# The output projection of a hybrid decoder step as seven block products instead of eight, with combined weights made on GpSimd

## The chip, the core and the metric

The kernel runs on one NeuronCore of a Trainium2 chip. The metric is device time in microseconds, the median of several executions; lower is better. The engines that matter here: TensorE (PE in the profile) multiplies, VectorE (DVE) and ScalarE (ACT) do elementwise work, GpSimd (POOL) does masks and memsets, and SyncE (SP) issues nearly all DMAs, in one queue, in order. On an engine an instruction that waits holds up all behind it.

## The reference, cut to what matters

One decoder layer: a combined input projection, a stick-breaking attention group and a gated linear attention (GLA) group, a SiLU gate on each, one output projection over the concatenated 2048 features, an RMS norm and a residual. There are 1024 prompt tokens (behind 16 meta tokens, whose output isn't returned) and 8 x 4 sample tokens.

```python
def branch_output(o_sb, sg, o_gla, gg, gla_norm_g, w_out):
    ...
    mixed = jnp.concatenate([o_sb * jax.nn.silu(sg), o_gla * jax.nn.silu(gg)], axis=-1)
    return mixed @ w_out
...
        x = x + rms_norm(branch_output(o_sb, sg, o_gla, gg, gla_norm_g[l], w_out[l]), norm_post_g[l])
```

`mixed @ w_out` is a product of 1024 (+ 32 sample) rows, 2048 features and 2048 columns in float32. The change is about this product.

## The kernel before, in words

Float32 operands are split into a rounded high part and a remainder, and each product is made of three matmuls: high by high, high by low, low by high.

On TensorE follow: input projections and attention of 8 heads (`head`, `attend`), then the GLA groups, then the paged values of the samples, with the 16 gate groups (`gate_group`) in between. A gate group multiplies by a weight block, applies SiLU, multiplies by the branch output and stores 128 features of the mixed activations for all tokens in a DRAM buffer `md[g]` (L402). The last two gate groups, 14 and 15, stand directly ahead of the output projection.

Side work is written as Python generators that a `Weaver` advances: each `W.beat()` in the main loop lets due generators emit their next instructions; `yield n` and `spawn(gen, delay)` count beats, and a beat of the input projections is six matmuls. The place on an engine's queue is then settled, when the program is built, by a scheduler that takes priorities (`urgent()`) and its own idea of when operands are ready. During the heads the generator `z_feed` has VectorE multiply 512 pages of cached keys by the sample queries (L376), paced at one page every two beats; GpSimd then only masks the diagonal attention tiles (L488, L504).

The output projection runs over two halves of 512 tokens (the first with the 32 samples as 544 columns). For each of 16 blocks of 128 output columns and each pair of feature blocks, `weight_chunk` loads 128 x 256 weights (L177, through three buffers), ScalarE rounds them (L181) and VectorE makes the remainder (L182). Weights are stationary, the activations of the half (`mix`, 272 or 512 tokens wide) stream past them (L1269 to L1271). `y_tok` transposes each finished block back to token rows (L1207), takes squares and multiplies by the gain. `finish0` adds the residual of the first half and stores it (L1233 to L1236) while the second half is multiplied; `finish1` does so for the second half (L1260, L1262), in two groups of tokens, for which the last two column blocks are kept back.

## Time and profile before

| | us |
|---|---|
| median of 3 runs | 2215.75 (2213.62 to 2221.52) |
| profiled execution | 2214.65 |
| span of that execution | 2212.9 |
| TensorE busy | 2150.0 (97%) |
| VectorE busy | 1593.0 (72%) |
| ScalarE busy | 1059.4 (48%) |
| GpSimd busy | 87.2 (4%) |

The span is what the profile covers; the time of the same execution is 1.75 us longer. Matmuls overlap, and their ends are modelled, so the sum of their durations isn't the time that they cost: the distance between starts is. A row of the groups reads: line, engine, operation, output<-inputs, shapes, count | busy us, mean ns of one | idle time of the engine just before them, and what ended most of it. A row of a stretch reads: start and end, length, busy us (and instructions) of PE, PEld (weight loads), DVE, ACT and POOL, the clock that TensorE was granted, the mean busy share of the 16 DMA engines, GB/s. A row of the chain reads: start, length, what; the chain follows the work that ended last back to what released it. A row of the timeline reads: start, length, engine, line, operation. SPq is SyncE's DMA queue.

### The profile page before, as it was taken

The numbers are of one execution on the slowest core, as the hardware profiler recorded it, in microseconds if no ns is written. First come the engines' busy times: TensorE is split into PE (matmuls) and PEld (weight loads), VectorE is DVE, ScalarE is ACT, GpSimd is POOL, SyncE is SP. The second block draws the span as 40 slices with busy tenths as digits, with TensorE's granted clock in tenths as the row PEclk, the third lists the DMA queues.
The fourth block names the chain that finished last, engine by engine and source line by source line (L and its number), as shares of the span: only waits on it lengthen the run. The fifth ranks groups of instructions, "written<-read, shape, count | busy, mean of one in ns | idle before, by whom it ended". The sixth has DMA issues, their size and how long they took to land. (4 is left out here: it accounts for less than half of the span.)

```text
span 2212.9 us, 46718 instructions
## 1 busy us (share of the span) xinstructions
PE 2150.0 (97%) x13712; PEld 1988.2 (90%) x13712; DVE 1593.0 (72%) x6809; ACT 1059.4 (48%) x2900; POOL 87.2 (4%) x299
## 2 busy tenths in 40 slices
...
GB/s 190 63 75 104 83 106 94 102 105 80 108 97 95 105 80 126 108 74 106 102 89 114 83 116 82 90 161 194 201 193 193 191 179 142 86 84 170 238 96 134
DMA packets 411299, 267.53 MB, mean 121 GB/s; under 512 B 49378, under 2 KB 393890, under 8 KB 409890
## 3 DMA queue, kind: packets, MB, share of 16 engines
...
q8 instruction: 108, 1.77, 0.3%
...
## 5 line engine op out<-in xcount | busy, mean ns | idle before, releaser
L376 DVE SCALAR_TENSOR_TENSOR jk<-kp,qb 128x128 f32<-128x128 f32 x2048 | 486.9, 287 | 40.9 <-DMA kp<-in_cache_k_dram 38.0
L286 PE MATMUL acc_g<-hT,wh_g 128*128 128x368 f32 (+2 forms) x768 | 258.0, 336 | 0.2
L287 PE MATMUL acc_g<-hT,wh_g 128*128 128x368 f32 (+2 forms) x768 | 247.6, 322 | 0.0
L288 PE MATMUL acc_g<-hT,wl_g 128*128 128x368 f32 (+2 forms) x768 | 246.9, 322 | 0.0
L1269 PE MATMUL oacc<-mx,wh_o 128*128 128x272 f32 (+1 forms) x736 | 238.8, 325 | 6.3 <-ACT wh_o L181 4.4
L1271 PE MATMUL oacc<-mx,wl_o 128*128 128x272 f32 (+1 forms) x736 | 235.5, 320 | 0.0
L1270 PE MATMUL oacc<-mx,wh_o 128*128 128x272 f32 (+1 forms) x736 | 234.8, 319 | 0.2 <-DVE mx L1186 0.2
L182 DVE TENSOR_TENSOR wl_o<-wr_o,wh_o 128x256 fp32r<-128x256 f32 x240 | 101.4, 425 | 152.4 <-ACT wh_o L181 146.3
L286 PEld LDWEIGHTS acc_g<-hT,wh_g 128*128 128x128 f32 x768 | 144.2, 188 | 33.6 <-issue 21.8
L376 DVE DVE_READ_ACCUMULATOR jk<-kp,qb 128x1 f32 x2048 | 166.0, 81 | 0.0
L181 ACT CAST wh_o<-wr_o 128x256 fp32r<-128x256 f32 x240 | 96.7, 405 | 138.7 <-PE oacc L1270 100.9
L1269 PEld LDWEIGHTS oacc<-mx,wh_o 128*128 128x128 f32 x736 | 139.1, 189 | 17.8 <-ACT wh_o L181 6.9
L1271 PEld LDWEIGHTS oacc<-mx,wl_o 128*128 128x128 f32 x736 | 138.6, 188 | 10.2 <-DVE wl_o L182 1.3
L1270 PEld LDWEIGHTS oacc<-mx,wh_o 128*128 128x128 f32 x736 | 138.9, 189 | 8.6 <-DVE mx L1186 0.5
L287 PEld LDWEIGHTS acc_g<-hT,wh_g 128*128 128x128 f32 x768 | 144.4, 188 | 1.1 <-issue 0.4
L288 PEld LDWEIGHTS acc_g<-hT,wl_g 128*128 128x128 f32 x768 | 144.3, 188 | 0.4 <-issue 0.4
L286 PE MATMUL acc_gv<-hT,wh_gv 128*128 128x384 f32 (+1 forms) x384 | 128.7, 335 | 0.0
L286 PE MATMUL acc_k<-hT,wh_k 128*128 128x378 f32 (+1 forms) x384 | 127.8, 333 | 0.0
L181 ACT CAST wh_g<-wr_g 128x256 fp32r<-128x256 f32 x128 | 51.7, 404 | 155.4 <-PE acc_g L287 140.1
L286 PE MATMUL acc_q<-hT,wh_q 128*128 128x368 f32 (+2 forms) x384 | 125.6, 327 | 0.0
L288 PE MATMUL acc_gv<-hT,wl_gv 128*128 128x384 f32 (+1 forms) x384 | 125.4, 327 | 0.0
L287 PE MATMUL acc_k<-hT,wh_k 128*128 128x378 f32 (+1 forms) x384 | 125.2, 326 | 0.0
(399 smaller groups left out, 5904.6 us busy)
## 6 DMA issues: line engine op xcount, KB each, us to landing
kp<-in_cache_k_dram SPq DMA_DIRECT2D x512, 64.0 KB
...
wr_o<-in_w_out_dram SPq DMA_DIRECT2D x256, 128.0 KB
...
wr_g<-in_w_in_dram SPq DMA_DIRECT2D x128, 128.0 KB
...
```

The lines of the kernel that those rows point to most:

```text
L181: act.copy(wh, raw[:])
L182: vec.tensor_tensor(wl, raw[:], wh.bitcast(F32), ALU.subtract)
L286: mm(acc[c][:, :n], wh[:, k2, :], hh[k][:, lo:hi], start=(k == 0), stop=False)
L287: mm(acc[c][:, :n], wh[:, k2, :], hl[k][:, lo:hi], start=False, stop=False)
L288: W.mark = mm(acc[c][:, :n], wl[:, k2, :], hh[k][:, lo:hi], start=False, stop=(k == NK - 1)).ins
L376: ins = vec.scalar_tensor_tensor(jk[:], kp[:], 1.0, qbs[h, b][:, t, :], ALU.mult, ALU.mult, accum_out=zt[:, t, NPG - 1 - i:NPG - i])
L1269: mm(o_, wh[:, k2, :], mh[:, lo:hi], start=(k == 0), stop=False)
L1270: mm(o_, wh[:, k2, :], ml[:, lo:hi], start=False, stop=False)
L1271: mm(o_, wl[:, k2, :], mh[:, lo:hi], start=False, stop=(k == NK - 1))
```

## The change

The output projection is now a block product by Strassen's method in Winograd's form. Activations A are cut into four quarters: two halves of 512 tokens by two halves of 1024 features; weights B into four quarters of 1024 features by 1024 columns. Seven products of a 512 x 1024 and a 1024 x 1024 matrix give what eight gave: 1 and 2 are quarters times quarters (A11 B11, A12 B21), 3 and 4 have a combined activation or weight, 5 to 7 have both. The sample rows don't take part: they are multiplied in the plain way, as 64 extra stationary columns (high and low parts of 32 rows), with the uncombined weight quarters that products 1, 2, 7 and 3 hold.

The parts:

- **Combined weights.** A new generator `weight_forms` starts 120 beats into the heads. In 16 rounds of 44 beats it loads four blocks of 128 x 512 weights (256 KB each), GpSimd makes four differences in place, and four blocks go out to DRAM buffers `td`. Each instruction is tied to the matmul emitted last (`spread`).
- **Gate groups 14 and 15** run ahead of the projection's pools, and the weight pool `wp` is closed after them; the projection's tiles are allocated anew. The sample columns of `md` are loaded early, as soon as a group is stored.
- **Forms.** `form(p)` loads the quarters of the activations that product p needs, combines them on VectorE (two of the sums are also stored and fetched again for later products), splits them and writes them over the slots of a finished product.
- **Products.** Activations are now stationary (128 features x 128 tokens) and weights stream, 512 columns wide. A `step(p, q)` is one product over one half of its columns: 8 feature blocks x 4 token tiles x 3 matmuls, into four PSUM banks of six in rotation. Weights come in chunks of 128 x 512 through three raw buffers and a ring of four split ones. The ring's index is the counter `turn`, which each `gain` load advances too (also in `sample_y`, which stands behind the steps of products 2 and 3).
- **Sums.** `take` adds a bank to the running sums in token rows; no transposes are left. Products 1 and 2 share banks, as do 6 and 7, and 5 and 3. The first token half is complete after product 3, and `finish0` and `finish_samples` are emitted from there on; the second half is complete with the fourth product, whose second column half has its weights kept (`kept`) and runs one token tile after another, each followed by `finish1`.

```diff
-    wp = ctx.enter_context(tc.tile_pool(name="wp", bufs=3))
+    wp_cm = tc.tile_pool(name="wp", bufs=3, side="right")
+    wp = wp_cm.__enter__()
...
+    td = [dram.tile([P, 8, 1024], F32, name=f"td{j}") for j in range(4)]
+    sd = [[dram.tile([P, 512], F32, name=f"sd{j}_{k}") for k in range(8)] for j in range(2)]
...
+    def spread(ins):
+        if W.mark is not None:
+            tc.add_manual_dep(ins.ins, W.mark.name, NOSYNC, reason="spread")
+    def weight_forms():
+        for k in range(8):
+            for q in range(2):
+                t = dk.tile([P, 4, 512], F32, tag="tf", bufs=1, name=f"tf{k}_{q}")
+                for i, (r, c) in enumerate(((0, 0), (0, 1), (1, 1), (1, 0))):
+                    r0, c0 = 1024 * r + k * P, 1024 * c + q * 512
+                    spread(nc.sync.dma_start(t[:, i, :], w_out[0, r0:r0 + P, c0:c0 + 512]))
+                    yield 4
+                yield 4
+                for i, a, b in ((0, 1, 0), (1, 1, 2), (2, 2, 0), (3, 3, 2)):
+                    spread(pool.tensor_tensor(t[:, i, :], t[:, a, :], t[:, b, :], ALU.subtract))
+                    yield 1
+                for j, i in enumerate((0, 2, 1, 3)):
+                    yield 4
+                    spread(nc.sync.dma_start(td[j][:, k, q * 512:(q + 1) * 512], t[:, i, :]))
...
         W.spawn(z_feed(lambda n: 2), lasting=True)
+        W.spawn(weight_forms(), 120, lasting=True)
         for h in range(HEADS):
...
+    small = [late.tile([P, 8, NSMP], F32, name=f"small{i}") for i in range(2)]
+    def load_small(c):
+        for k in range(8):
+            nc.sync.dma_start(small[c][:, k, :], md[8 * c + k][:, SEQ:TOUT])
+    gate_group(14)
+    load_small(0)
+    vec.tensor_tensor(small[0][:], small[0][:], osmp[:], ALU.mult)
+    gate_group(15)
+    wp_cm.__exit__(None, None, None)
...
+        REGION = dict(zip("ABC", ((0, 1, 2, 3), (6, 7, 8, 9), (10, 11, 12, 13))))
+        HOME = {1: "A", 2: "B", 6: "C", 7: "A", 5: "B", 3: "C", 4: "A"}
...
+        def quarter(r, c, k, nm):
+            t = raw(f"q{r}{c}_{k}_{nm}")
+            nc.sync.dma_start(t[:], md[8 * c + k][:, 512 * r:512 * r + 512])
+            return t[:]
...
+        def combined(p, k):
+            if p in (1, 2, 4):
+                return quarter(p == 4, p > 1, k, p)
+            if p == 6:
+                x, y_, z = quarter(1, 0, k, p), quarter(1, 1, k, p), quarter(0, 0, k, p)
+                vec.tensor_tensor(x, x, y_, ALU.add)
+                nc.sync.dma_start(sd[0][k][:], x)
+                vec.tensor_tensor(z, x, z, ALU.subtract)
+                nc.sync.dma_start(sd[1][k][:], z)
+                return z
+            if p == 5:
+                return stored(0, k)
+            x, y_ = (quarter(1, 0, k, p), quarter(0, 0, k, p)) if p == 7 else (quarter(0, 1, k, p), stored(1, k))
+            vec.tensor_tensor(x, x, y_, ALU.subtract)
+            return x
+        def form(p, gap):
+            sample = {1: 0, 2: 1, 7: 0, 3: 1}.get(p)
+            if p == 3:
+                vec.tensor_tensor(small[1][:], small[1][:], small[0][:], ALU.add)
+            for i in range(4):
+                t = slot(REGION[HOME[p]][i], f"f{p}_{i}")
+                for j in range(2):
+                    k = 2 * i + j
+                    f = t[:, j * 1024:(j + 1) * 1024].rearrange("p (s n) -> p s n", s=2)
+                    split(f[:, 0], f[:, 1], combined(p, k))
+                    forms[p, k] = f
+                    if sample is not None:
+                        f = t[:, 2048 + 64 * j:2112 + 64 * j]
+                        split(f[:, 0:NSMP], f[:, NSMP:64], small[sample][:, k, :])
+                        smp[p, k] = f
+                    if gap:
+                        yield gap
...
+        def weights(p, q, k, dst=None):
+            with urgent():
+                if dst is None:
+                    j = next(turn) % 4
+                    dst = [t[:, j * 512:(j + 1) * 512] for t in ring]
+                wh, wl = dst
+                r = op.tile([P, 512], F32, tag="wr", bufs=3, name=f"wr{p}{q}_{k}")[:]
+                if p <= 3:
+                    r0, c0 = (1024 if p > 1 else 0) + P * k, (1024 if p == 3 else 0) + 512 * q
+                    src = w_out[0, r0:r0 + P, c0:c0 + 512]
+                else:
+                    src = td[{5: 0, 6: 1, 7: 2, 4: 3}[p]][:, k, q * 512:(q + 1) * 512]
+                nc.sync.dma_start(r, src)
+                act.copy(wh, r)
+                vec.tensor_tensor(wl, r, wh.bitcast(F32), ALU.subtract)
+            return wh, wl
+        ring += [slot(4 + i, f"ring{i}") for i in range(2)]
+        for _ in form(1, 0):
+            pass
+        W.spawn(form(2, 1))
+        W.spawn(form(6, 3), 10)
...
+        def gain(b):
+            t = op.tile([P, 512], F32, tag="gpost", bufs=2, name=f"gpost{b}_{next(turn)}")
+            nc.sync.dma_start(t[:], norm_post_g[0, b * 512:(b + 1) * 512].partition_broadcast(P))
+            return t
...
+        def finish0():
+            r = scale((0, 1, 2, 3))
             for i in range(4):
+                for b in range(4):
+                    o = sums_[i, b]
+                    for f in range(2):
+                        fs = slice(f * 256, (f + 1) * 256)
+                        x = stage(f"xr{i}_{b}_{f}")[:, :256]
+                        nc.sync.dma_start(x, x_prompt[0, i * P:(i + 1) * P, b * 512 + f * 256:b * 512 + (f + 1) * 256])
+                        vec.scalar_tensor_tensor(o[:, fs], o[:, fs], r[:, i:i + 1], x, ALU.mult, ALU.add)
+                    nc.sync.dma_start(y_prompt[0, i * P:(i + 1) * P, b * 512:(b + 1) * 512], o)
...
+        def finish1(i):
+            r = scale((4 + i,))
+            for b in range(4):
+                cs = slice(b * 512, (b + 1) * 512)
+                o = sums_[4 + i, b]
+                vec.scalar_tensor_tensor(o, o, r[:, 0:1], xr[i][:, cs], ALU.mult, ALU.add)
+                nc.sync.dma_start(y_prompt[0, 512 + i * P:512 + (i + 1) * P, cs], o)
+        def product(bk, t, p, k, w, first, last):
+            wh, wl = w
+            ah, al = (forms[p, k][:, s_, t * P:(t + 1) * P] for s_ in range(2))
+            mm(bk[:], ah, wh, start=first and k == 0, stop=False, skip_group_check=True)
+            mm(bk[:], ah, wl, start=False, stop=False, skip_group_check=True)
+            mm(bk[:], al, wh, start=False, stop=last and k == 7, skip_group_check=True)
+        def step(p, q, banks, first, last):
+            c = {1: 0, 2: 0, 7: 1, 3: 1}.get(p)
+            if p in (1, 7):
+                SB[c, q] = ops.tile([P, 512], F32, tag="S", bufs=2, name=f"sc{c}{q}")
+            for k in range(8):
+                w = weights(p, q, k)
+                for t in range(4):
+                    product(banks[t], t, p, k, w, first, last)
+                if c is not None:
+                    s_ = SB[c, q][:64]
+                    mm(s_, smp[p, k], w[0], start=p in (1, 7) and k == 0, stop=False, skip_group_check=True)
+                    mm(s_, smp[p, k], w[1], start=False, stop=p in (2, 3) and k == 7, skip_group_check=True)
+                W.beat()
+            for t in range(4):
+                take(p, q, t, banks[t])
+            if p in (2, 3):
...
+        AFTER = {(1, 1): lambda: W.spawn(form(7, 2)), (2, 1): lambda: W.spawn(form(5, 4)), (6, 1): lambda: W.spawn(form(3, 2)),
+                 (7, 1): lambda: W.spawn(form(4, 4))}
+        for pa, pb in ((1, 2), (6, 7), (5, 3)):
+            for q in range(2):
+                if pa != 6:
+                    need(q if pa == 1 else 2 + q)
+                banks = [bank(f"b{pa}{q}_{t}") for t in range(4)]
+                for p in (pa, pb):
+                    step(p, q, banks, p == pa, p == pb)
+                    AFTER.get((p, q), lambda: None)()
+        W.spawn(finish0())
+        W.spawn(finish_samples())
+        for q in range(2):
+            need(q)
+        xr = []
+        for i in range(4):
+            xr.append(slot(REGION["C"][i], f"xr{i}")[:, :D].bitcast(F32))
+            nc.sync.dma_start(xr[i], x_prompt[0, 512 + i * P:512 + (i + 1) * P])
+        step(4, 0, [bank(f"b40_{t}") for t in range(4)], True, True)
+        keep = [slot(REGION["B"][i], f"keep{i}") for i in range(4)]
+        kept = [weights(4, 1, k, [keep[k // 2][:, (2 * (k % 2) + i) * 512:(2 * (k % 2) + i + 1) * 512] for i in range(2)])
+                for k in range(8)]
+        for t in range(4):
+            bk = bank(f"b41_{t}")
+            for k in range(8):
+                product(bk, t, 4, k, kept[k], True, True)
+                W.beat()
+            take(4, 1, t, bk)
+            finish1(t)
...
-    nc = bacc.Bacc("TRN2", target_bir_lowering=False, num_devices=1)
+    nc = bacc.Bacc("TRN2", target_bir_lowering=False, num_devices=1, dynamic_dma_scratch_size=1024)
```

Three places show how the instructions now stand. In the rows of the queues, `L` is a line of the kernel in question, then operation, output<-inputs, shape, and what the instruction waits for by engine or DMA lane.

SyncE's queue at the end of gate group 15, before: `wr_o` are weights of the output projection, `mraw` parts of the mixed activations, `md_124` the last of the 16 buffers.

```order
L177 DMA wr_o_0_6_31286<-in_w_out_dram 128x2x128 [waits DMAHW3_49,DMAHW1_49,DVE_49]
L402 DMA md_124<-gs_16_31031 128x368 [waits DMAHW2_49,DVE_49]
L177 DMA wr_o_0_7_31304<-in_w_out_dram 128x2x128 [waits DMAHW4_49,DVE_49]
L1178 DMA mraw_0_0_31340<-md_109 128x256 [waits DVE_49]
L402 DMA md_124<-gs_384_31050 128x384 [waits DMAHW5_49,DVE_49]
```

The same place now: `wr` are weights of the first product, `qFalseFalse_1` quarters of A11.

```order
L1282 DMA wr_0_31394<-in_w_out_dram 128x512 [waits DMAHW2_49,DMAHW3_49,DVE_49,DMAHW5_49,PE_49,Pool_49]
L1282 DMA wr_1_31419<-in_w_out_dram 128x512
L1282 DMA wr_2_31443<-in_w_out_dram 128x512 [waits DMAHW4_49]
L418 DMA go_768_31296<-od_108 128x304 [waits DVE_49]
L428 DMA md_124<-gs_16_31260 128x368 [waits DVE_49]
L1223 DMA qFalseFalse_1_31321<-md_109 128x512 [waits DMAHW7_49]
L1282 DMA wr_3_31468<-in_w_out_dram 128x512 [waits DMAHW2_49,DMAHW0_49,DVE_49]
L428 DMA md_124<-gs_384_31279 128x384 [waits DMAHW1_49,DVE_49]
```

Before, seven weight loads of the first block and 15 of 16 activation parts stood ahead of these stores. Now the first weight load waits for TensorE; the count in its wait is that of the last matmul of gate group 15. The first quarter of A11 stands behind the first store of `md_124`.

GpSimd's queue in the heads, before: masks of attention tiles.

```order
L488 AFFINE_SELECT X_1_5_3347<-X_1_5_3347 127x126 [waits DVE_49,Pool_49]
L504 AFFINE_SELECT Y_1_6_3466<-Y_1_6_3466 127x126 [waits DVE_49,Activation_49,Pool_49]
L488 AFFINE_SELECT X_1_4_3446<-X_1_4_3446 127x102 [waits DVE_49,Pool_49]
L504 AFFINE_SELECT Y_1_5_3552<-Y_1_5_3552 127x126 [waits Activation_49]
L504 AFFINE_SELECT Y_1_4_3652<-Y_1_4_3652 127x102 [waits Activation_49]
```

Now, with the differences of weights (`tf`) in it:

```order
L514 AFFINE_SELECT X_1_4_3471<-X_1_4_3471 127x102 [waits DVE_49,Pool_49]
L405 TENSOR_TENSOR tf_0_3077<-tf_0_3077 128x512 [waits DMAHW2_49,DMAHW0_49]
L530 AFFINE_SELECT Y_1_5_3578<-Y_1_5_3578 127x126 [waits Activation_49]
L405 TENSOR_TENSOR tf_0_3077<-tf_0_3077 128x512 [waits DMAHW0_49,Pool_49]
L405 TENSOR_TENSOR tf_0_3077<-tf_0_3077 128x512 [waits Pool_49]
L405 TENSOR_TENSOR tf_0_3077<-tf_0_3077 128x512 [waits DMAHW4_49,Pool_49]
L530 AFFINE_SELECT Y_1_4_3681<-Y_1_4_3681 127x102 [waits Activation_49]
```

The differences stand between the masks, three of them in one piece here.

SyncE's queue where the results of the first token half leave, before: residual (`xr`) and result (`y`) between the weights of the second half.

```order
L1233 DMA xr_2_34248<-in_x_prompt_dram 128x256 [waits DMAHW4_49]
L177 DMA wr_o_2_2_34297<-in_w_out_dram 128x2x128 [waits DMAHW5_49,DVE_49]
L1236 DMA out_dram<-y_0_31170 128x2048 [waits DMAHW6_49,DVE_49]
L177 DMA wr_o_2_3_34312<-in_w_out_dram 128x2x128 [waits DMAHW7_49,DVE_49]
L177 DMA wr_o_2_4_34327<-in_w_out_dram 128x2x128 [waits DMAHW2_49,DMAHW0_49,DVE_49]
```

Now, some rows of the end, where no weights are left in between; L1376 loads residual, L1378 stores the first half (`c`, `y`), L1405 the second (`u`).

```order
L1378 DMA out_dram<-y_1_2_32717 128x512 [waits DMAHW4_49,DVE_49]
L1376 DMA xr_2_0_34015<-in_x_prompt_dram 128x256 [waits DMAHW5_49]
L1376 DMA xr_2_1_34018<-in_x_prompt_dram 128x256 [waits DMAHW6_49]
L1378 DMA out_dram<-c_0_31385 128x512 [waits DMAHW7_49,DVE_49]
L1378 DMA out_dram<-c_1_31386 128x512 [waits DMAHW0_49,DVE_49]
L1376 DMA xr_3_0_34025<-in_x_prompt_dram 128x256 [waits DMAHW1_49]
L1376 DMA xr_3_1_34028<-in_x_prompt_dram 128x256 [waits DMAHW2_49]
L1405 DMA out_dram<-u_0_31590 128x512 [waits DMAHW3_49]
L1378 DMA out_dram<-y_0_3_32412 128x512 [waits DMAHW4_49,DVE_49]
```

Behind the load of the last kept weight stand, in this manner, 28 of the 32 residual loads of the first half and 14 of its 16 stores, mixed at the end with the 16 stores of the second half.

241 lines of the change are left out of this document (97 added, 144 removed).

## The prediction

> **What bounds the kernel now.** I read the page's first two parts, then busy time by stretches, then the chain that ended last, then groups by shape, then single instructions at the two ends of the output projection.
>
> ```profile
> PE 2150.0 (97%) x13712; PEld 1988.2 (90%) x13712; DVE 1593.0 (72%) x6809; ACT 1059.4 (48%) x2900; POOL 87.2 (4%) x299
> ```
>
> ```profile
> 1810.00:1830.00 20.00, 17.86 (x124) 16.65 (x123) 8.80 (x24) 9.31 (x31) 0.00 (x0) 0.91 0.50 144
> 2028.00:2104.00 76.00, 72.17 (x323) 57.47 (x322) 37.03 (x101) 29.52 (x103) 0.00 (x0) 1.00 0.77 244
> 2120.00:2160.00 40.00, 40.00 (x185) 33.09 (x184) 16.22 (x44) 17.94 (x64) 0.00 (x0) 1.00 0.32 93
> 400.00:800.00 400.00, 398.36 (x2420) 376.32 (x2419) 311.38 (x1630) 227.66 (x583) 35.65 (x116) 1.00 0.37 97
> ```
>
> The columns after the stretch are PE, PEld, DVE, ACT, POOL, the granted clock, the DMA share and GB/s. TensorE is the bound in the heads (398.36 of 400 us) and in the output projection, so the time is matmul issue time plus the few holes. Overlapping matmuls make "busy" useless as a price; what one costs is the distance between equal places, here the transposes that close each column block in the chain:
>
> ```profile
> 1872.17 0.44 PE yp L1207 x4
> 1884.74 0.44 PE yp L1207 x4
> ...
> 2131.29 0.44 PE yp L1207 x4
> 2142.67 0.44 PE yp L1207 x4
> ```
>
> A block of the first token half takes 12.57 us (96 matmuls of 272 columns and the transposes), one of the second half 11.38 us (48 of 512 columns). A matmul of 512 columns costs (11.38 - 0.44)/48 = 0.228 us.
>
> ```profile
> L1269 PE MATMUL oacc<-mx,wh_o 128*128 128x272 f32 x512 | 149.5, 292 | 2.5 <-ACT mx L1185 1.2 <-ACT wh_o L181 0.6 <-ACT yt L1274 0.6
> L1269 PE MATMUL oacc<-mx,wh_o 128*128 128x512 f32 x224 | 89.3, 399 | 3.8 <-ACT wh_o L181 3.8
> L1269 PE MATMUL oacc<-mx,wk 128*128 128x256 f32 x64 | 18.5, 292 | 0.6 <-ACT wk L181 0.6
> ```
>
> ```profile
> 1801.26 0.30 PE L288 MATMUL acc_g<-hT,wl_g 128*128 128x304 f32 x1
> ...
> 2199.99 0.28 PE L1271 MATMUL oacc<-mx,wk 128*128 128x256 f32 x1
> ```
>
> These are the last matmul of the last gate group and the last product of the projection. From 1801.5 to 2200.3 the projection holds TensorE for 398.8 us; to the span's end at 2212.9 there are another 12.6.
>
> **The change, term by term.**
>
> (a) Matmuls. Removed: three lines times 512 + 224 + 64 matmuls, and 144 transposes. Added: 7 products x 2 column halves x 8 k x 4 token tiles x 3 = 1344 matmuls of 512 columns and 4 x 2 x 8 x 2 = 128 for the samples, also 512 wide. 1472 x 0.228 = 335.6 us, against 398.8: 63 us less. Each keeps one weight load of 128 columns, as before, so I see no reason for another spacing.
>
> (b) The start. Before, output weights come through the same buffers as the gates' and are there when the last gate matmul ends. In the first pair of queue pieces above this is gone. The new buffers lie where the closed pool's were, so the first load waits for TensorE's last gate matmul; and the first quarter of the mixed activations stands behind a store (L428) that waits for the gate's chain on VectorE. What that chain takes is in the trace, as the three stores of the last group on the same queue, beside two loads:
>
> ```profile
> 1805.07 0.42 SPq L402 DMA_DIRECT2D md<-gs  x1
> ...
> 1807.17 0.32 SPq L402 DMA_DIRECT2D md<-gs  x1
> ...
> 1809.66 0.46 SPq L402 DMA_DIRECT2D md<-gs  x1
> ```
>
> ```profile
> 1833.53 2.58 DMA mraw<-md
> ...
> 2079.63 5.69 DMA wr_o<-in_w_out_dram
> ```
>
> ```profile
> L461 ACT CAST hi_s<-X 127x512 fp32r<-127x512 f32 x48 | 29.6, 616 | 0.3
> ...
> L462 DVE TENSOR_TENSOR lo_s<-X,hi_s 127x512 fp32r<-127x512 f32 x48 | 33.0, 688 | 2.1 <-ACT hi_s L461 2.0
> ```
>
> So the first quarter is asked for at 1805.5, lands 2.6 to 5.7 us later (3.5 taken, the queue being half empty), is cast in 0.62: products begin at about 1809.6, 8.1 us after the gates. The second quarter, behind the 1807.17 store and two weights, costs about 0.8 more. The old hole of 1810 to 1830 went with a clock of 0.91, 1.8 us; I add that, and take off 1.1 for five sample products that run in the hole. Term: +9.5 us (5 to 14).
>
> (c) Between products. Evacuation, weight splits and the new forms are about 0.6 to 0.7 us for 512 columns; VectorE has some 330 of them, 220 us under 335 of TensorE, and of four banks the first three are done before the step ends. Two things show. The index of the four-deep weight ring also advances with every gain load; three stand before the last product, so its first weight goes into the slot of the weight last used and must be cast and subtracted after the step: 2 us. And transfers: in the first four steps (14 x 8 x 0.228 = 25.5 us each) 8.4 MB of weights, 2.1 of A12, 10.5 of loads and stores for the sums, about 2 of the next form and 1.6 of gains make 24.6 MB in 102 us, 241 GB/s. The stretch from 2028 to 2104 is the nearest row: 244 GB/s at a share of 0.77, 323 matmuls where the rate of 2120 to 2160 (52 a block of 11.38 us) needs 70.7 us of 76, so 7% lost. 7% of 102 and of the 25.5 us step in which the residual rows are fetched is 9 us. Term: +10 (2 to 20).
>
> (d) The end. Before, the first half's results leave while the second half is multiplied for 16 more blocks. Now (third pair of pieces above) no weights are left to come. Behind the last weight stand 28 of the 32 residual loads and nearly all 16 stores of the first half, then the last 16 stores: one queue in order, every store waiting for VectorE. From the start of the last product's first half these remain: a 1.05 MB row tile, 0.5 of weights, 2.1 of kept weights, 0.5 of gains, 4.2 of residual, 4.2 and 4.2 of results, 0.5 for the samples: 17.3 MB. At the 244 GB/s above that is 71 us. TensorE has 2 x 96 x 0.228 = 43.8 us there, and after the last matmul the old tail is
>
> ```profile
> 2204.21 5.13 DVE L1260 SCALAR_TENSOR_TENSOR y<-y,r_y,xr 128x512 f32<-128x512 f32 x6
> ```
>
> six such operations behind transposes that are gone; with four instead of six I count 10 of the 12.6 us. So the end lies between 54 (transfers hidden) and 71; I take 65, nearer to the row with the same kinds of transfer. That is 21 us above TensorE's work (10 to 28).
>
> (e) The heads. 64 subtractions of 512 columns on GpSimd, 33.6 MB more traffic over 704 beats of about 1 us, 45 GB/s on the 97 of 400 to 800; the share rises from 0.37 to about 0.54, which I cost at nothing for the weights. GpSimd's queue also carries the masks of the attention tiles, and three subtractions can stand in front of one (second pair of pieces).
>
> ```profile
> L504 POOL TENSOR_SCALAR_AFFINE_SELECT Y<-Y 127x126 f32<-127x126 f32 x48 | 14.4, 301 | 158.5 <-ACT Y L502 134.7 <-DVE jk L376 20.5 <-issue 3.3
> ...
> L620 POOL MEMSET qbz<- 128x480 f32 x1 | 0.5, 510 | 0.0
> ...
> L376 DVE SCALAR_TENSOR_TENSOR jk<-kp,qb 128x128 f32<-128x128 f32 x1636 | 390.3, 287 | 37.6 <-DMA kp<-in_cache_k_dram 35.2 <-DMA qb<-qsd 2.0
> ```
>
> No two-input GpSimd operation is in the trace. A write of 480 columns (0.51 us) bounds it below, 301 ns per 126 columns scaled to 512 (1.2 us) is the nearest row that reads and writes; I take 1.2. A mask behind three of them is 3.6 us late, on a chain with 4 beats of room (masks of X) or 6 (of Y) less about 2.3 us of its own work: 1.7 to 3.7 us of cover. So 0 to 1.9 us, 0.7 taken, reach TensorE in each of the 12 groups that fall into the attention: +8 us (0 to 40). The Trainium skill, "GPSIMD Engine Reference", section 3.1, gives a two-input fp32 add as 1.96 times VectorE's; with 688 ns of L462 that would be an estimate of 1.35 us and a term of about 13 in place of 8. No run here shows it yet.
>
> Sum: 1801.5 + 8 (e) + 9.5 (b) + 335.6 (a) + 10 (c) + 21 (d) = 2185.6 us of span. The profiled execution was 2214.65 against a span of 2212.9, so 1.75 more: 2187 us. The median shown, 2215.75, is 1.1 above that execution, less than 0.5% (11 us), which is about what this kernel's measurement can tell from no change.
>
> **Rivals.**
>
> Everything is covered (17%): masks not late, transfers at the end and in the first steps hidden. 1801.5 + 0 + 6 + 335.6 + 2 + 10 = 2155, so 2157. For it: transfers reached 244 GB/s with only 7% lost; against it: 17.3 MB in 54 us would be 320.
>
> Heads held up (13%), ends slower. GpSimd's subtractions and VectorE's products of two SBUF operands (L376, 390 us of it) block each other, subtractions stretch, masks and the stores that wait for GpSimd on SyncE's queue come late. If all four subtractions of a group (4 x 1.2 us) reach TensorE in 16 groups, 77 us: 2187 - 8 + 77 = 2256. It decides from 2.3 us a group on (37 us). For it: masks already waited 20.5 us behind L376. Against it: TensorE lost 1.6 of 400 us there with VectorE 78% busy, so there is room on both. The Trainium skill, "SBUF — State Buffer", section "Who interferes with whom", says that a VectorE instruction with two SBUF inputs and a GpSimd instruction that reads SBUF exclude each other for a whole instruction; by that rule each subtraction can also stop VectorE for its length. The trace of before has no such pair to show it.
>
> Transfers bound the whole projection (12%), no gain or slower. It moves 76 MB (29.4 weights, 23.1 quarters and sums loaded, 4.2 stored, 2.6 gains, 16.8 residual and results). At 244 GB/s that is 313 us and stays under TensorE; at 180, because every store waits in order, 424: 1801.5 + 8 + 424 + 2 = 2235. It decides at about 192.
>
> The main case has 55%, its own range 2168 to 2204; 3% is left for others (a matmul spacing above 0.228: each hundredth is 15 us). Faster by over 0.5% (below 2204.7): nearly all of the main case, the first rival, and a little of the milder late cases: 0.74. Within: 0.10, from their middle. Slower: 0.16, from the last two rivals' hard ends and the rest. The range leaves one in ten on either side: below it the better half of the first rival, above it the late cases past their deciding point, so 2157 to 2218.
>
> **What the profile after would show.** Right: 512-column matmuls 0.228 us apart; a hole of 7 to 10 us behind the last gate matmul at about 1810; a DMA share near 0.8 in the first 100 us of the projection and over the last 60; the last matmul more than 12 us before the end, or itself late, with stores in the chain. Wrong: the last gate matmul later than 1840 (heads), TensorE busy below 90% through the middle of the projection (transfers), or GpSimd's subtractions over 2.5 us each.

## The result and the profile after

The changed kernel takes 2225.77 us (median of 11 runs, 2223.59 to 2230.63) against 2216.18 for the kernel before on the same chips (11 runs): a ratio of 1.0044, 95% interval 1.0033 to 1.0055. It is slower by 0.44%, which lies inside the 0.5% that the prediction counted as no change. 2187 was forecast.

The profiled execution has a span of 2225.0 us, 12.1 longer than the 2212.9 of before. Two places tell where it went: the last matmul of the last gate group, which ends the heads and the GLA part, and the end.

| | before | after | forecast |
|---|---|---|---|
| last gate matmul ends | 1801.5 | 1839.2 | 1809.5 |
| from there to the end of the span | 411.4 | 385.8 | 376.1 |
| span | 2212.9 | 2225.0 | 2185.6 |

The output stage is 25.6 us shorter. The stages ahead of it, whose matmuls the change does not touch, are 37.7 us longer. First the totals of the page, then five stretches of the changed kernel (columns as in the prediction):

```profile
PE 2109.9 (95%) x12640; PEld 1898.4 (85%) x12640; DVE 1667.0 (75%) x6712; ACT 1001.5 (45%) x2568; POOL 177.5 (8%) x364
```

```profile
400.00:800.00 400.00, 384.23 (x2295) 364.63 (x2293) 319.02 (x1547) 219.15 (x558) 71.12 (x136) 0.99 0.47 127
1840.00:1855.00 15.00, 11.17 (x35) 6.78 (x36) 9.60 (x19) 8.13 (x17) 0.00 (x0) 0.77 0.84 258
1870.00:1885.00 15.00, 12.03 (x47) 9.13 (x46) 9.15 (x14) 7.72 (x14) 0.00 (x0) 0.89 0.89 286
1885.00:1900.00 15.00, 15.00 (x67) 11.75 (x67) 7.25 (x11) 4.09 (x7) 0.00 (x0) 1.00 0.92 298
2199.00:2225.00 26.00, 0.01 (x1) 0.00 (x0) 17.54 (x46) 2.55 (x10) 0.00 (x0) 0.58 0.81 283
```

In the stretch of 400 us inside the heads TensorE was busy for 398.36 us before and is for 384.23 now. VectorE's busy time has risen from 311.38 to 319.02 there, though it issues fewer instructions in the stretch (1547 against 1630): the instructions themselves have become longer. GpSimd's instructions and the page products, by tile and by line:

```profile
L405 POOL TENSOR_TENSOR tf<-tf x64: 1250/1326/3267, 239.2 to 1124.7; 128x512 f32<-128x512 f32 x64
```

```profile
L379 DVE SCALAR_TENSOR_TENSOR jk<-kp,qb x2048: 259/284/1458, 134.3 to 1516.5; 128x128 f32<-128x128 f32 x187
```

The three numbers are the shortest, median and longest in ns. A subtraction takes 1326 ns, not far from the 1.2 us assumed, but up to 3267. One of VectorE's page products, which never took more than 499 ns before, takes 1458.

The rest of the profile after, on TensorE's timeline, from the last gate matmul to the last product:

```profile
1838.95 0.30 PE L291 MATMUL acc_g<-hT,wl_g 128*128 128x304 f32 x1
1843.28 0.69 PE L1427 MATMUL sc<-ring,f 128*64 128x512 f32 x1 [4.03 <-ACT ring L1283]
...
1846.69 0.79 PE L1410 MATMUL b<-ring,f 128*128 128x512 f32 x1
...
1875.73 0.80 PE L1410 MATMUL b<-ring,f 128*128 128x512 f32 x1 [2.97 <-ACT u L1321]
...
2197.71 0.39 PE L1411 MATMUL b<-keep,f 128*128 128x512 f32 x1
...
2198.62 0.39 PE L1412 MATMUL b<-keep,f 128*128 128x512 f32 x1
```

The hole behind the gates is there, products follow each other in 0.2275 us (0.91 us for the last four), and the last one ends at 2199.0, 26.0 us before the span does. The chain ends in residual loads and the final additions:

```profile
2206.72 3.84 DMA xr<-in_x_prompt_dram
2211.07 0.60 DVE u L1347
2212.75 1.41 DVE u L1404 x2
```

### The profile page after: what moved, and what is told of

It is laid out like the page before. It is cut to its first block, busy times and chain, and to the rows that moved or that the text cites. A ratio compares the mean times of both kernels' runs of the same rounds, so it can differ in the third digit from the quotient of the medians.

```text
span 2225.0 us, 43958 instructions
## 1 busy us (share of the span) xinstructions
PE 2109.9 (95%) x12640; PEld 1898.4 (85%) x12640; DVE 1667.0 (75%) x6712; ACT 1001.5 (45%) x2568; POOL 177.5 (8%) x364
## 5 line engine op out<-in xcount | busy, mean ns | idle before, releaser
L379 DVE SCALAR_TENSOR_TENSOR jk<-kp,qb 128x128 f32<-128x128 f32 x2048 | 512.8, 299 | 39.2 <-DMA kp<-in_cache_k_dram 33.5
L1410 PE MATMUL b<-ring,f 128*128 128x512 f32 x416 | 164.6, 397 | 9.7 <-ACT u L1321 5.1
L1411 PE MATMUL b<-ring,f 128*128 128x512 f32 x416 | 163.9, 394 | 0.3 <-DVE ring L1284 0.3
L1412 PE MATMUL b<-ring,f 128*128 128x512 f32 x416 | 163.2, 393 | 0.0
L1284 DVE TENSOR_TENSOR ring<-wr,ring 128x512 fp32r<-128x512 f32 x104 | 71.4, 688 | 92.1 <-ACT ring L1283 91.5
L289 PE MATMUL acc_gv<-hT,wh_gv 128*128 128x384 f32 (+1 forms) x384 | 128.9, 336 | 4.5 <-ACT gq L959 4.5
L289 PE MATMUL acc_q<-hT,wh_q 128*128 128x368 f32 (+2 forms) x384 | 126.2, 329 | 0.0
L290 PE MATMUL acc_gv<-hT,wh_gv 128*128 128x384 f32 (+1 forms) x384 | 125.8, 328 | 0.0
L291 PE MATMUL acc_k<-hT,wl_k 128*128 128x378 f32 (+1 forms) x384 | 125.2, 326 | 0.0
L290 PE MATMUL acc_q<-hT,wh_q 128*128 128x368 f32 (+2 forms) x384 | 124.5, 324 | 0.0
L291 PE MATMUL acc_q<-hT,wl_q 128*128 128x368 f32 (+2 forms) x384 | 124.2, 324 | 0.0
L1283 ACT CAST ring<-wr 128x512 fp32r<-128x512 f32 x104 | 64.2, 619 | 126.2 <-PE sc L1427 56.8
```

What stands on the lines that cost most here:

```text
L289: mm(acc[c][:, :n], wh[:, k2, :], hh[k][:, lo:hi], start=(k == 0), stop=False)
L290: mm(acc[c][:, :n], wh[:, k2, :], hl[k][:, lo:hi], start=False, stop=False)
L291: W.mark = mm(acc[c][:, :n], wl[:, k2, :], hh[k][:, lo:hi], start=False, stop=(k == NK - 1)).ins
L379: ins = vec.scalar_tensor_tensor(jk[:], kp[:], 1.0, qbs[h, b][:, t, :], ALU.mult, ALU.mult, accum_out=zt[:, t, NPG - 1 - i:NPG - i])
L1283: act.copy(wh, r)
L1284: vec.tensor_tensor(wl, r, wh.bitcast(F32), ALU.subtract)
```

## The experiments

Two questions were put: what makes the heads 37.7 us longer, and what holds the end. For the first there were three theories. A: a subtraction stands in GpSimd's row, with its wait for a load, ahead of the masks that TensorE needs (the prediction's own mechanism, at a larger size). B: the 33.6 MB of traffic and 128 issues. C: VectorE and GpSimd shut each other out while a subtraction runs (the prediction's second rival). All runs in one table; "last gate" is the start of the last gate matmul, and VectorE's busy time is that of the whole span; both are of the one profiled execution, the median is of all runs. The kernels of e1, e2, e3, e5, e6 and e7 leave out some or all of the weight forms, that of e11 the residual, so their results are not the layer's.

| kernel | last gate, us | VectorE busy, us | span, us | median, us | ratio to before (95%) |
|---|---|---|---|---|---|
| before | 1801.3 | 1593.0 | 2212.9 | 2216.2 | 1 |
| changed | 1838.9 | 1667.0 | 2225.0 | 2225.8 | 1.0044 (1.0033 to 1.0055) |
| e3, no weight forms | 1799.1 | 1615.6 | 2187.4 | 2195.1 | 0.9902 (0.9885 to 0.9919) |
| e1, transfers only | 1807.0 | 1616.2 | 2188.4 | 2195.3 | 0.9901 (0.9884 to 0.9917) |
| e2, subtractions only | 1837.0 | 1670.8 | 2226.2 | 2228.2 | 1.0046 (1.0030 to 1.0063) |
| e5, memsets only | 1805.6 | 1615.0 | 2192.0 | 2193.4 | 0.9890 (0.9874 to 0.9907) |
| e7, copies only | 1826.9 | 1658.7 | 2213.0 | 2214.1 | 0.9981 (0.9967 to 0.9995) |
| e6, half subtractions | 1813.9 | 1640.2 | 2200.6 | 2199.3 | 0.9919 (0.9898 to 0.9939) |
| e10, subtractions apart | 1842.1 | 1670.7 | 2229.6 | 2231.6 | 1.0060 (1.0037 to 1.0083) |
| e4, on VectorE | 1817.9 | 1650.2 | 2200.9 | 2200.4 | 0.9922 (0.9897 to 0.9948) |
| e9, on VectorE, apart | 1819.0 | 1649.3 | 2201.4 | 2202.9 | 0.9935 (0.9914 to 0.9955) |
| e8, formed late | 1806.2 | 1666.3 | 2226.6 | 2227.6 | 1.0046 (1.0028 to 1.0063) |
| e11, no residual loads | 1834.9 | 1667.4 | 2208.3 | 2216.5 | 0.9997 (0.9986 to 1.0009) |
| e12, residual early | 1811.3 | 1650.6 | 2194.3 | 2200.2 | 0.9925 (0.9909 to 0.9942) |
| e13, wide residual | 1815.6 | 1648.0 | 2194.1 | 2195.5 | 0.9894 (0.9880 to 0.9908) |
| e14, second row | 1816.0 | 1651.2 | 2202.9 | 2202.7 | 0.9930 (0.9917 to 0.9944) |

### What the new output stage is worth alone (e3)

```diff
-        W.spawn(weight_forms(), 120, lasting=True)
...
-                    src = td[{5: 0, 6: 1, 7: 2, 4: 3}[p]][:, k, q * 512:(q + 1) * 512]
+                    r0, c0 = P * k + (1024 if p > 5 else 0), 512 * q
+                    src = w_out[0, r0:r0 + P, c0:c0 + 512]
```

> No weight forms at all in the heads (products 4 to 7 read plain blocks of the weights): what the new output stage is worth by itself. All theories: heads as before the change, last gate matmul at 1800 to 1805, output stage 384 to 388 as in the changed kernel, time 2186 to 2192. If the last gate matmul stays above 1810, something else in the change (slots, pools, the order) slows the heads.

1799.1 and a ratio of 0.9902: without weight forms the heads are as before, and the seven products are a gain of 1%. The whole loss belongs to the forms. (e8 below has the same heads and reached 1806.2, so the last gate of a single execution can be 7 us off; runs at 1799 to 1807 are not told apart.) The median, 2195.1, lies 3 us above the time expected.

### The transfers alone, the subtractions alone (e1, e2)

```diff
-                for i, a, b in ((0, 1, 0), (1, 1, 2), (2, 2, 0), (3, 3, 2)):
-                    spread(pool.tensor_tensor(t[:, i, :], t[:, a, :], t[:, b, :], ALU.subtract))
+                for i in range(4):
                     yield 1
```

> The subtractions are left out (the raw blocks of the weights are stored, so products 4 to 7 multiply other weights); the 64 loads, the 64 stores and their beats stay. In the changed kernel the last gate matmul stood at 1839 us instead of 1801. Theory A (the place: a subtraction, with its wait for a load, stands in GpSimd's row ahead of masks that TensorE needs): the loss goes with the subtractions, last gate matmul at 1802 to 1810, time 2189 to 2197. Theory B (the traffic: 33.6 MB more, and 128 more issues in SyncE's row): the loss stays, 1830 to 1839, time 2217 to 2226. Theory C (VectorE and GpSimd shut each other out while a subtraction runs): as A.

```diff
+        t = dk.tile([P, 4, 512], F32, tag="tf", bufs=1, name="tf")
+        pool.memset(t[:], 0.0)
...
-                    spread(nc.sync.dma_start(t[:, i, :], w_out[0, r0:r0 + P, c0:c0 + 512]))
                     yield 4
...
-                    spread(nc.sync.dma_start(td[j][:, k, q * 512:(q + 1) * 512], t[:, i, :]))
```

> The transfers are left out: the same 64 subtractions run on a tile that was filled with zeros once, and products 4 to 7 read plain blocks of the weights. Nothing that a subtraction waits for is late here. Theory A: if the 1.4 us of each subtraction are what counts, last gate matmul at 1825 to 1839 and time 2212 to 2226; if it is the wait for late loads at the head of GpSimd's row, 1806 to 1818 and 2193 to 2205. Theory B: 1801 to 1806, time 2188 to 2193. Theory C: 1825 to 1839, with single VectorE instructions drawn out to over 1 us as in the changed kernel.

The transfers cost at most 8 us (1807.0; by the medians, 2195.3 against the 2195.1 of e3, nothing), the subtractions all of it (1837.0, with no transfer to wait for; the median, 2228.2, is 2 us above the range). B falls. So does the half of A that put the loss down to waiting for late loads: in the changed kernel GpSimd did wait 127.9 us for them, and e2, which does not wait, loses as much.

### The same time on GpSimd without reading (e5)

```diff
-                    spread(pool.tensor_tensor(t[:, i, :], t[:, a, :], t[:, b, :], ALU.subtract))
+                    spread(pool.memset(t[:, 0:3, :], 0.0))
```

(against the kernel of e2)

> As the run with subtractions alone, but each subtraction is a memset of 1536 columns on GpSimd (the 1024 columns of the memset at line 1074 took 0.94 us, so about 1.4 us each): it holds GpSimd as long and reads nothing. Theory A (GpSimd's row): like the run with subtractions alone, within 3 us. Theory C (shutting out between two engines that read SBUF): last gate matmul at 1801 to 1808, and no VectorE instruction of line 379 over 0.6 us. Theory B: 1801 to 1806.

64 memsets of 1383 ns, at the same places in GpSimd's row (but for a few neighbours that changed places) as 64 subtractions of 1456 ns on average, leave the last gate at 1805.6, among the runs without forms. GpSimd's row is held equally long ahead of the masks, so A falls: its place in the row is not what costs. VectorE's busy time says where the difference lies: 1615.0 us with memsets, 1670.8 with subtractions. Here is the same moment in both kernels, four operations in a run on GpSimd and what VectorE does meanwhile (timeline; a start, a length, engine, line). With subtractions:

```profile
299.62 6.17 POOL L405 TENSOR_TENSOR tf<-tf 128x512 f32<-128x512 f32 x4
```

```profile
299.75 1.45 DVE L185 TENSOR_TENSOR wl_q<-wr_q,wh_q 128x256 fp32r<-128x256 f32 x1 [0.71 <-ACT wh_q L184]
301.12 1.38 DVE L379 SCALAR_TENSOR_TENSOR jk<-kp,qb 128x128 f32<-128x128 f32 x1
...
302.44 0.68 DVE L487 TENSOR_TENSOR lo_a<-Y,hi_a 127x512 fp32r<-127x512 f32 x1
303.04 1.39 DVE L379 SCALAR_TENSOR_TENSOR jk<-kp,qb 128x128 f32<-128x128 f32 x1
...
304.57 1.37 DVE L379 SCALAR_TENSOR_TENSOR jk<-kp,qb 128x128 f32<-128x128 f32 x1
```

With memsets:

```profile
298.63 5.71 POOL L405 MEMSET tf<- 128x1536 f32 x4
```

```profile
298.77 0.43 DVE L185 TENSOR_TENSOR wl_q<-wr_q,wh_q 128x256 fp32r<-128x256 f32 x1 [0.92 <-ACT wh_q L184]
299.12 0.29 DVE L379 SCALAR_TENSOR_TENSOR jk<-kp,qb 128x128 f32<-128x128 f32 x1
...
299.37 0.69 DVE L487 TENSOR_TENSOR lo_a<-Y,hi_a 127x512 fp32r<-127x512 f32 x1
```

The same split (line 185) takes 1.45 us instead of 0.43, the same page product 1.37 to 1.39 instead of 0.29: each stands until a subtraction is over. (All 29 page products of e2 that took over 0.6 us, and all 25 of the changed kernel, end 0.15 us after the end of a subtraction.) The split at 302.44 started together with a subtraction and kept its 0.68 us; that subtraction was the longest of the four (1.84 us). In 6 us VectorE gets a handful of instructions through. Which instructions this hits is seen in the groups of both kernels from 230 to 960 us (count | busy us, mean ns of one | idle time of VectorE ahead of them, and what ended it). Without forms (e3), then with subtractions alone (e2):

```profile
L379 DVE SCALAR_TENSOR_TENSOR jk<-kp,qb 128x128 f32<-128x128 f32 x1144 | 274.4, 289 | 29.8 <-DMA kp<-in_cache_k_dram 29.4
L511 DVE SCALAR_TENSOR_TENSOR X<-z,bias,X 127x512 f32<-127x512 f32 x42 | 31.5, 751 | 15.5 <-ACT X L510 15.1
...
L488 DVE TENSOR_TENSOR lo_s<-X,hi_s 127x512 fp32r<-127x512 f32 x42 | 28.9, 689 | 1.8 <-ACT hi_s L487 1.7
```

```profile
L379 DVE SCALAR_TENSOR_TENSOR jk<-kp,qb 128x128 f32<-128x128 f32 x1080 | 291.7, 319 | 17.4 <-DMA kp<-in_cache_k_dram 17.1
L487 DVE TENSOR_TENSOR lo_s<-X,hi_s 127x512 fp32r<-127x512 f32 x42 | 33.3, 792 | 1.7 <-ACT hi_s L486 1.7
L510 DVE SCALAR_TENSOR_TENSOR X<-z,bias,X 127x512 f32<-127x512 f32 x42 | 31.4, 749 | 14.7 <-ACT X L509 14.5
```

(Line 511 of e3 is line 510 of e2, 488 is 487.) The page product and the split, which read two tiles in SBUF, went from 289 to 319 and from 689 to 792 ns. The other, of the same size, reads `z` in PSUM and only one tile in SBUF, and stayed at 750. That is C, and it is what the Trainium skill states in "SBUF — State Buffer", section "Who interferes with whom": a VectorE instruction with two SBUF inputs contends with a GpSimd instruction that reads SBUF, not with one that only writes it. These runs agree (1.38 us against 0.29 under subtractions, no change under memsets), and show how long the hold lasts: to the end of GpSimd's instruction.

How this reaches TensorE is seen in its waits from 100 to 1160 us (who waits, for whom: us in total, times, longest). Before, then in the changed kernel:

```profile
PE z L498 <- DVE lo_s L462: 0.2, 1, 0.2
```

```profile
PE z L524 <- DVE lo_s L488: 10.1, 12, 2.3
PE z L523 <- ACT hi_s L487: 5.1, 3, 4.4
...
PE acc_v L289 <- DVE q L618: 4.5, 4, 1.7
```

TensorE waits for splits that come late in VectorE's row. In the same stretch all its waits for VectorE add up to 6.6 us with memsets (e5) and 25.2 with subtractions (e2); its waits for GpSimd stay at 4.2 and 3.6.

### One operand, half the columns, further apart (e7, e6, e10)

```diff
-                    spread(pool.tensor_tensor(t[:, i, :], t[:, a, :], t[:, b, :], ALU.subtract))
+                    spread(pool.tensor_copy(t[:, 2:4, :], t[:, 0:2, :]))
```

(e7, against the kernel of e2)

> As the run with subtractions alone, but each is a GpSimd copy of 1024 columns from one half of the tile to the other: it reads SBUF with one operand instead of two, and products 4 to 7 read plain blocks. If GpSimd shuts VectorE out whenever it reads SBUF, the loss is that of the subtractions by the copy's length: at 1.3 us each, last gate matmul at 1825 to 1840 and VectorE instructions of line 379 drawn out to over 1 us. If only two operands do it: 1799 to 1807, time 2187 to 2195, and line 379 stays under 0.6 us.

A copy reads one operand and shuts out as well: the last gate at 1826.9, and in the run of four copies at the same place VectorE is drawn out to the copy's length:

```profile
299.60 4.76 POOL L405 COPY tf<-tf 128x1024 f32<-128x1024 f32 x4
```

```profile
299.74 1.17 DVE L185 TENSOR_TENSOR wl_q<-wr_q,wh_q 128x256 fp32r<-128x256 f32 x1 [0.49 <-ACT wh_q L184]
300.83 1.12 DVE L379 SCALAR_TENSOR_TENSOR jk<-kp,qb 128x128 f32<-128x128 f32 x1
```

```diff
-                    spread(pool.tensor_tensor(t[:, i, :], t[:, a, :], t[:, b, :], ALU.subtract))
+                    spread(pool.tensor_tensor(t[:, i, :256], t[:, a, :256], t[:, b, :256], ALU.subtract))
```

(e6, against the kernel of e2)

> As the run with subtractions alone (64 of them, no transfers, plain blocks in products 4 to 7), with 256 columns each instead of 512. If the price goes with the time that GpSimd subtracts, half of the 38 us of the whole ones: last gate matmul at 1815 to 1821, time 2203 to 2209. If each subtraction has a fixed price (a hand-over, a place in the row), nearly all of it: 1830 to 1837. If only a long one hurts because it outlasts the slack: 1800 to 1808.

1813.9, just under the range given for a price that goes with time, and a median of 2199.3, 4 us under it; a fixed price for each subtraction is excluded. The four doses stand in a row, though not in proportion. GpSimd's time in these instructions (58.0 us in e6, 71.0 in e7, 91.4 in the changed kernel, 93.1 in e2) goes with VectorE's busy time above the 1615 to 1616 of e1, e3 and e5 (25, 43, 51, 55 us) and with the last gate against 1803, the middle of the runs without GpSimd reading (11, 24, 36, 34 us). By that, some 40 to 70% of what VectorE loses reaches TensorE. By the medians, against 2194.3, the middle of those of e1, e3 and e5, the four cost 5, 20, 31 and 34 us, or 20 to 60%. The shorter subtractions of e6 hold GpSimd for 62% of e2's time and cost a third of e2's loss or less: it may be that part of a short hold is taken up.

```diff
-                    yield 4
+                    yield 2
...
                     spread(pool.tensor_tensor(t[:, i, :], t[:, a, :], t[:, b, :], ALU.subtract))
-                    yield 1
+                    yield 6
                 for j, i in enumerate((0, 2, 1, 3)):
-                    yield 4
+                    yield 1
```

(e10, against the changed kernel; the first pair is in the loop over the loads)

> The changed kernel with its GpSimd subtractions six beats (about 8 us) apart instead of one, at the same pace of rounds; the result is the reference's. If the loss goes with the sum of the time in which VectorE is shut out, nothing changes: last gate matmul at 1832 to 1841, time 2218 to 2228. If it is the run of four (5.6 to 6 us) that TensorE's supply does not outlast, and a single one of 1.3 us is taken up by VectorE's idle time: 1808 to 1822, time 2190 to 2206.

1842.1 and a median of 2231.6, just above the ranges given for no change: further apart, the subtractions cost no less. The run is weaker than it was meant to be, since late loads pushed many of them together again: of the 48 distances between starts within a round, 20 are still under 2 us, against 30 in the changed kernel (median 4.8 us against 1.8). Still, if VectorE's slack swallowed single holes of 1.3 us, a part of the loss should have gone.

### The subtractions on VectorE (e4, e9)

```diff
-                    spread(pool.tensor_tensor(t[:, i, :], t[:, a, :], t[:, b, :], ALU.subtract))
+                    spread(vec.tensor_tensor(t[:, i, :], t[:, a, :], t[:, b, :], ALU.subtract))
```

> The 64 subtractions run on VectorE instead of GpSimd; loads, stores and beats stay, and the result is the reference's. A VectorE subtraction of this size took 0.6 to 0.7 us in the changed kernel (line 1237), so VectorE gets 38 to 45 us of work in stretches where it is 77% busy. If the loss is the shutting out (one VectorE instruction let through for each 1.3 us of GpSimd's subtraction), it goes, and what is left is what VectorE's idle time does not take up: last gate matmul at 1802 to 1820, time 2189 to 2207. If VectorE's own time is what is short, so that any 32 us added there cost the same, last gate matmul at 1830 to 1845 and 2217 to 2232.

e9 adds to this the beats of e10:

```diff
-                    yield 4
+                    yield 2
...
-                    yield 1
+                    yield 6
...
-                    yield 4
+                    yield 1
```

> The subtractions on VectorE, six beats (about 8 us) apart instead of one, the loads and stores closer together, so that a round still takes 44 beats; the result is the reference's. With four in a row (2.7 us) the last gate matmul stood at 1818 us against 1807 with the transfers alone. If it is the run of four that VectorE's row has no slack for: 1807 to 1812, time 2188 to 2195. If VectorE's total counts: 1815 to 1821, time 2197 to 2204.

VectorE does one in 686 ns, about half of GpSimd's 1326 (the Trainium skill, "GPSIMD Engine Reference", section 3.1, has 1.96 for an add; here it is 1.93). 44 us of work for VectorE cost the heads 15 us, where 91 us on GpSimd cost 36 (by the medians 6 and 31), and the kernel becomes faster than before: 0.9922. Taking them apart, which here put all of them over 2 us from each other, gains nothing (1819.0).

### Forming the weights late (e8)

```diff
-        W.spawn(weight_forms(), 120, lasting=True)
...
+                first, *rest = {1: ((0, 0),), 2: ((1, 0),), 3: ((1, 1),), 5: ((0, 1), (0, 0)), 7: ((0, 1), (1, 1)),
+                                6: ((1, 1), (0, 1), (0, 0)), 4: ((1, 0), (2, 0))}[p]
+                r = block(*first, "wr", 3)
+                for j_, b_ in enumerate(rest):
+                    vec.tensor_tensor(r, r, block(*b_, "fr", 5), ALU.add if j_ else ALU.subtract)
```

(`block` loads one block; row 2 is the stored sum of product 6)

> No weight forms in the heads; products 4 to 7 load the blocks that they need in the output stage and VectorE subtracts them there (80 more instructions of 0.7 us, 56 us on an engine that is 52% busy there, 21 MB more loaded and 4 MB stored), and the result is the reference's. Heads as without forms: last gate matmul at 1798 to 1803. Output stage 386 us if TensorE covers the added work, up to 410 if the loads bind while two or three blocks are waited for: time 2186 to 2212.

Heads as without forms (1806.2, 3 us above the range), but 420 us of output stage: 10 more than the worst expected. In VectorE's row a subtraction waits for its second block, and with it the additions that read the banks; a stretch of the middle, and one of VectorE's and two of TensorE's waits in the stage:

```profile
1950.00:2000.00 50.00, 43.15 (x175) 32.93 (x174) 31.99 (x51) 11.86 (x20) 0.00 (x0) 0.93 0.81 264
```

```profile
DVE wr L1284 <- DMA wr<-in_w_out_dram: 42.3, 30, 4.3
```

```profile
PE b L1414 <- DVE y L1333: 7.3, 3, 5.7
PE b L1414 <- DVE u L1335: 5.8, 2, 4.4
```

VectorE stands 42.3 us in 30 waits for blocks, TensorE 13.1 us for the additions (L1333, L1335) and 2.7 for splits. That stretch starts 175 matmuls where 0.2275 us apiece would give 220.

### The end (e11 to e14)

```diff
-                        nc.sync.dma_start(x, x_prompt[0, i * P:(i + 1) * P, b * 512 + f * 256:b * 512 + (f + 1) * 256])
-                        vec.scalar_tensor_tensor(o[:, fs], o[:, fs], r[:, i:i + 1], x, ALU.mult, ALU.add)
+                        vec.scalar_tensor_tensor(o[:, fs], o[:, fs], r[:, i:i + 1], o[:, fs], ALU.mult, ALU.add)
...
-            nc.sync.dma_start(xr[i], x_prompt[0, 512 + i * P:512 + (i + 1) * P])
```

(e11, against the changed kernel)

> The changed kernel without the loads of the input that is added to the result (8.4 MB of the 17.3 MB that cross after the last product begins; each instruction adds the product itself instead). Heads as in the changed kernel, last gate matmul at 1834 to 1842. If the transfers bind the end, it shrinks from 26 us after the last matmul to 9 to 16: time 2209 to 2217. If the chain of squares, scale and stores of the last tiles binds: 21 to 26 us, time 2221 to 2227.

The end after the last matmul shrinks from 26.0 to 14.5 us, and the time by 9. From the start of product 4 to the end 17.4 MB cross in the changed kernel and 12.1 here. That is 5.3 MB less and not the 8.4 of the expectation, since three of the four loads of the lower tiles are issued 7 to 20 us ahead of product 4. So residual loads hold the end. Which of them?

```diff
+        def residual():
+            for i in range(4):
+                yield 2
+                xr.append(slot(REGION["B"][i], f"xr{i}")[:, :D].bitcast(F32))
+                nc.sync.dma_start(xr[i], x_prompt[0, 512 + i * P:512 + (i + 1) * P])
+
+        AFTER[5, 1] = lambda: W.spawn(residual())
...
-        keep = [slot(REGION["B"][i], f"keep{i}") for i in range(4)]
+        keep = [slot(REGION["C"][i], f"keep{i}") for i in range(4)]
```

(e12, against e4; the old loads are gone)

> The subtractions on VectorE, and the 4.2 MB of input for the lower four tiles loaded during the last step of product 3 instead of beside product 4 (they take the slots of product 5's forms, and the kept weights take those of product 3's); the result is the reference's. Last gate matmul at 1815 to 1820 as before with VectorE. If transfers bind the end, as the run without the residual loads says, 13.1 MB instead of 17.3 MB cross after product 4 begins, at 244 GB/s 54 us instead of 71: the tail after the last matmul shrinks from 24 us to 12 to 18, time 2188 to 2196. If the moved loads hold up the weights of product 3 instead, the last step of it grows by what the end gains: 2198 to 2204.

Both expectations fell: the end did not shrink, and the last step of product 3 did not grow (the time, that of e4, lies in the second range, but not for its reason). The loads of the lower tiles, 4.2 of the 8.4 MB of residual, now lie 23 to 26 us earlier, counted from product 4, and hold up nothing (358.0 us from the last gate matmul's end to the last product's, against 358.6 in e4), yet the end is 24.7 us, against 24.1. The run says less than it was meant to. In e4 these loads are issued from 2112.8 to 2132.0, and product 4 begins at 2132.5; so of the 17.3 MB from there on only about 1 went, and behind the last matmul as much is left as before.

```diff
-                        x = stage(f"xr{i}_{b}_{f}")[:, :256]
-                        nc.sync.dma_start(x, x_prompt[0, i * P:(i + 1) * P, b * 512 + f * 256:b * 512 + (f + 1) * 256])
-                        vec.scalar_tensor_tensor(o[:, fs], o[:, fs], r[:, i:i + 1], x, ALU.mult, ALU.add)
+                    x = raw(f"xr{i}_{b}")[:]
+                    nc.sync.dma_start(x, x_prompt[0, i * P:(i + 1) * P, b * 512:(b + 1) * 512])
+                    vec.scalar_tensor_tensor(o, o, r[:, i:i + 1], x, ALU.mult, ALU.add)
```

(e13, against e4)

> The subtractions on VectorE, and the residual of the upper four tiles loaded and added in 16 pieces of 512 columns instead of 32 of 256: the same bytes, 16 issues fewer in SyncE's row behind the last weights, 16 VectorE instructions fewer. In the run without residual loads (36 issues and 8.4 MB fewer) the end after the last matmul fell from 26 to 14.5 us; in the run with 4.2 MB moved ahead (4 issues) it stayed at 25 against 24. If the bytes in flight bind the end: 23 to 26 us, time 2198 to 2203. If SyncE's row binds it (16 issues of 0.42 to 0.46 us): 16 to 19 us, time 2191 to 2196.

```diff
-                        nc.sync.dma_start(x, x_prompt[0, i * P:(i + 1) * P, b * 512 + f * 256:b * 512 + (f + 1) * 256])
+                        nc.scalar.dma_start(x, x_prompt[0, i * P:(i + 1) * P, b * 512 + f * 256:b * 512 + (f + 1) * 256])
```

(e14, against e4)

> The subtractions on VectorE, and the 32 residual loads of the upper four tiles issued by ScalarE instead of SyncE: same bytes, same pieces, 32 issues out of SyncE's row. If the bytes bind the end: 23 to 26 us after the last matmul, time 2198 to 2203. If SyncE's row binds it, 32 x 0.42 = 13 us are there to be had, less what ScalarE's own row loses by waiting for free tiles ahead of its squares: 13 to 20 us, time 2189 to 2197.

Half as many pieces (e13): an end of 19.1 us and 5 us less time. Another engine's row (e14): 26.2 us, and ScalarE's squares now wait behind its loads. ScalarE's waits from 2140 us on in e14:

```profile
ACT b L1346 <- DMA out_dram<-y: 8.6, 1, 8.6
...
ACT b L1346 <- DMA xr<-in_x_prompt_dram: 6.8, 2, 4.9
```

What crosses at the end in the six kernels:

| kernel | MB from the start of product 4 | MB after the last matmul | that end, us | GB/s in it |
|---|---|---|---|---|
| changed | 17.4 | 7.4 | 26.0 | 283 |
| e4 | 17.3 | 7.1 | 24.1 | 294 |
| e12 | 16.3 | 7.4 | 24.8 | 297 |
| e13 | 16.0 | 5.4 | 19.1 | 282 |
| e14 | 17.3 | 6.2 | 26.2 | 236 |
| e11 | 12.1 | 3.1 | 14.5 | 215 |

e13 changes more than the number of pieces. Its loads go through other tiles, of which five are free early, and so five of the 16 loads (1.3 MB) are issued at 2025 to 2038, some 100 us ahead of product 4. In the four kernels that load residual by SyncE alone the end goes with the MB that are left behind the last matmul, at 282 to 297 GB/s; so the bytes are not out. e14 has fewer of them than e4, and no shorter end. By their expectations e13 speaks for SyncE's row (16 to 19 us) and e14 for the bytes (23 to 26), and neither is clean. What e13 gains it may owe to the bytes that come early, to 16 issues fewer in SyncE's row, to fewer waits for pieces that are under way for 3.2 to 5.9 us each, or to the 3.4 us that VectorE saves with 16 additions of 0.75 us instead of 32 of 0.48. That stays open.

e13 is the best version found, and faster than both kernels: 2195.5 us, 0.9894 (0.9880 to 0.9908) of the kernel before. Its interval just overlaps that of e4, its last gate is 16 us behind that of e3, and e3 shows about the same time with no forms at all.

## Why the prediction was wrong, step by step

- (a) Matmuls: right. 1472 at 0.2275 us make 334.9 us, 335.6 was forecast.
- (b) The start: right. Products begin 7.4 us after the gates (8.1 forecast), and the clock fell in the hole (0.77 in 1840 to 1855), as it had in the hole of the kernel before (0.91 in 1810 to 1830). By 1855, 15.75 us after the gates, 35 matmuls had started, 34 fewer than at full rate: 7.8 us, 9.5 forecast.
- (c) Between products: too small. From the end of the gates to the end of the last matmul are 359.7 us; less 334.9 of matmuls and 7.8 of the start that leaves 17, where 10 stood in a range of 2 to 20. It came otherwise than the term had it, as transfers that slow the first four steps by 7%. The stretch at 1885 has a DMA share of 0.92 and 298 GB/s, and with 67 matmuls it runs at full rate. The loss sits where one step ends and the next begins: the stretches of 15 us from 1870, 1900, 1930 and 1960 start 47, 54, 55 and 50 matmuls, together 62 too few, or 14 us. What the term left out is ScalarE's row there. In the first product the casts of product 2's forms wait for their loads and stand ahead of the copies that read product 1's banks, into which product 2 adds. TensorE stood 2.97 us for one of these at 1875.7, in the quoted timeline, and the clock fell to 0.89 again; for such copies it stood 5.1 us in all, for ScalarE's squares of banks 2.6.
- (d) The end: too small by 5. It lies 70 us after the start of the last product's first half, at the upper bound of 54 to 71, 65 taken. Bytes and rate of that bound were right (17.4 MB at 247 GB/s, where 17.3 at 244 stood); the step that failed is that some 6 us of it were taken as hidden. Whether the bytes themselves or the rows that issue them set the end stays open (e11 to e14).
- (e) The heads: this step failed. "+8 us (0 to 40)" came as 37.7. The price of one subtraction was good (1.2 us taken, 1326 ns measured). The way from there to TensorE was wrong: it went through masks that come late behind three subtractions, and memsets of the same length at the same places (e5) show that this costs nothing that can be told from scatter. The beat was mis-sized too: from the first load to the last store 700 beats lasted 942 us, 1.35 us each where about 1 was taken, which by that sum gives the masks more cover still. The traffic, "cost at nothing", cost 8 us at most. What the sum lacked is that a subtraction stops VectorE's own work: VectorE was busy 51 us longer, and TensorE waited for its splits.
- The rival that came true was the second, at 13%: GpSimd and VectorE block each other. It had been held against it that TensorE lost only 1.6 of 400 us with VectorE 78% busy, "so there is room on both". That is idle time in a row that runs in order, filled with page products ahead of the splits that TensorE waits for. It takes up a part only: of 44 us of VectorE work in single pieces of 0.7 us, 6 to 16 us reached TensorE (e4, e9). The rival's own figure, 77 us for four subtractions in 16 groups, was twice what came, and its deciding point (37 us in the heads) was just met: hence a result near no change.
- The sum: 1839.2 (29.7 over) + 385.8 (9.7 over) = 2225.0 against 2185.6.

Of the signs named ahead, "the last gate matmul later than 1840" sat at its threshold (1839.2) and pointed to the right place; "subtractions over 2.5 us each" did not show the mechanism, since it is mostly VectorE that waits (the longest subtraction took 3267 ns, the median 1326).
